# Everything ahead of the experts in one hand-written order: modulation as matmuls, the state-space operators on VectorE, parameters loaded in long rows

## The chip, the core and the metric

One core of a Trainium2 chip runs the whole program. The time is the device time of that core in microseconds (us), the median of three runs. The engines are PE (TensorE matmul; PEld, its weight loads), DVE (VectorE), ACT (ScalarE), POOL (GpSimd) and SP, which here only issues DMAs.

## What is computed

One layer of a hybrid network on 512 latent rows and 256 context rows of 1024 columns, all in float32:

```python
m = silu(cond) @ w_mod + b_mod              # 6 x 1024 columns, for c; the first 2 x 1024 for c_ctx too
h = rmsnorm(x, norm1_g) * (1 + scale1) + shift1
z = h @ w_in                                # 256 columns u, 3 x 768 columns b, c, v
y = concat(s5(u), b * dwconv3(c * v))       # s5: two diagonal complex scans, glu
x = x + gate1 * (y @ w_out)
h = rmsnorm(x, norm2_g) * (1 + scale2) + shift2
# top group of 4, then 2 of its 4 experts: weights and indices from h
x = x + gate2 * sum_e gates[:, e] * ((silu(h @ w1[e]) * (h @ w3[e])) @ w2[e])   # 16 experts
out = rmsnorm(x, final_g)
```

## The kernel before, in words

**Precision.** A float32 product that matters is made of three matmuls of 128 rows by 512 columns (mm3, line 97), for which each operand is split in a high part (ACT, line 74) and a low one (a subtraction on DVE or POOL, line 75).

**Modulation.** w_mod has 6144 columns. The first 2048 (shift and scale of the first norm, for c and c_ctx) come in 16 loads of 512 KB in rows of 512 bytes (load_mod) and are multiplied with 128 by 128 matmuls of 2 columns (line 91, `b,sc`), turned on PE, and make Asc and modT (lines 249 to 252). The other 4096 columns are mod_rows (lines 719 to 751): for each of eight parts q of 512 columns, DVE multiplies half of the eight 128-row blocks by sc and adds them up (line 735), ACT and POOL do the other half (lines 739 to 742), and a matmul with ones (ones_f) sums over the partitions into a row that is the same on all partitions: mx2 (the gate), sh2, A2 (shift and scale of the second norm) and mx5.

**First norm and u.** x is normed and turned on PE, modulated as it leaves PSUM (ACT line 518, DVE line 520), split into H and L; two blocks of w_in give u, for x and for ctx.

**S5 operators.** From lambda, dt, B and C come powers of a_bar (apw), the input operator MinT (12 products and sums of 1024 elements per partition on DVE; cmul, lines 310 to 315), the phasors W (doubling steps on POOL, in s5_tables) and the output operator CA (24 operations of 576 elements on POOL). s5_scan takes u through them: matmuls, products, two scans per direction (lines 638 to 667), readout, gelu and glu.

**Conv blocks.** 18 blocks of 128 columns of w_in, six each of c, v and b: a load, a split (five of the b blocks on POOL), 24 matmuls, and DVE and ACT work on the result (lines 590 to 607).

**Order.** All of this is written as four generators that are advanced in turn (cv_, scan_, mods_, ins_); a scheduler that simulates the program places the instructions on each engine, with a few explicit constraints (issue_after). The expert section alone is in manual order for PE, DVE, ACT and POOL.

**Output projection and router.** wo_mm(n) does 16 steps of 12 matmuls (8 for each half of the columns): w_out is multiplied by mx2 on POOL (line 869), split, used. add_x adds x (line 920). XA = x * A2 (line 954, DVE); the rows go through PE to the logits (line 937); lg (line 966) starts the top-k chain of small DVE operations, which ends in the one-hot matrices OH (line 1009). With those PE gathers expert 0's rows (X0, `bank<-OH,b`), first_parts adds the shift and splits (lines 1056 to 1058). Four operations of 1024 elements (line 1176) scale x for the table td in DRAM, from which the later experts' rows are gathered (POOL, line 1024).

**Experts.** 192 loads of 512 KB go into a ring of 34 slots (load_to), each piece is split (split_to; the first seven among the last conv blocks and the steps of the output projection), each expert takes 72 large matmuls; its result is scattered to yd (POOL, line 1029). Then yd is read back and normed.

Of the kernel before, what the change touches and what calls it, by code (L numbers as in the profile page):

```python
# [7 lines left out]
F32 = mybir.dt.float32  # L8
# [6 lines left out]
CAP = 96  # L15
# [3 lines left out]
def layer_kernel(  # L19
# [79 lines left out]

    R_X = R_MIN = R_SBD = 0  # L100
# [10 lines left out]
    wm_slot = [at(R_RING + 4 * i, [8, 128]) for i in range(8)]  # L111
# [3 lines left out]
    Cr = at(R_SM + 2, [2, 2, 128])  # L115
# [6 lines left out]
    def load_mod(q):  # L122
        m = (q // 4 % 2) * 8 + q // 8 * 4 + q % 4
        D.dma_start(wm_slot[q % 8], dap(w_mod, m * 128, [[6144, 128], [6144 * 128, 8], [1, 128]]))
# [8 lines left out]
    s5_loads = []  # L133
    for ri, src in enumerate((s5_lambda_re, s5_lambda_im)):
        for d in range(2):
            r0 = (ri * 2 + d) * 8
            s5_loads.append((R2[r0:r0 + 8].rearrange("r (a p) -> r a p", a=2),
                             dap(src, d * 1024, [[64, 8], [512, 2], [1, 64]])))
    for g in range(2):
        s5_loads.append((LD[g * 64:(g + 1) * 64], dap(s5_log_dt, g * 8, [[0, 64], [16, 2], [1, 8]])))  # L140
    for ri, src in enumerate((s5_b_re, s5_b_im)):
        for d in range(2):
            for g in range(2):
                s5_loads.append((Bt[g * 64:(g + 1) * 64, ri, d],
                                 dap(src, d * 16384 + g * 8192, [[16, 64], [1024, 8], [1, 16]])))
    for ri, src in enumerate((s5_c_re, s5_c_im)):
        s5_loads.append((Cr[:, ri].rearrange("r d (a p) -> r (d a) p", a=2), dap(src, 0, [[64, 128], [8192, 4], [1, 64]])))
    s5_loads.append((vec2[0:16], dap(b_mod, 0, [[128, 16], [1, 128]])))
    s5_loads.append((vec2[16:24], dap(norm1_g, 0, [[128, 8], [1, 128]])))
    s5_loads.append((vec2[24:26], dap(b_glu, 0, [[128, 2], [1, 128]])))  # L150
    s5_loads.append((vec2[26:44], dap(conv_w, 0, [[128, 18], [1, 128]])))

    def small(n):
        for _ in range(n):
            if s5_loads:
                o_, i_ = s5_loads.pop(0)
                D.dma_start(o_, i_)

    S.dma_start(vec[0:8], dap(c, 0, [[128, 8], [1, 128]]))
    S.dma_start(vec[8:16], dap(c_ctx, 0, [[128, 8], [1, 128]]))  # L160
    load_mod(0)
    load_mod(1)
    small(4)
    load_mod(2)
    small(2)
    load_mod(3)
    small(4)
    load_mod(4)
    load_x(0)
    small(4)  # L170
    load_mod(5)
    load_x(1)
    small(9)
    load_mod(6)
    load_mod(7)
    load_x(2)
# [39 lines left out]
    warm = ct([1, 1], F32, "warm")  # L216
    S.activation(warm, ones_f[0:1, 0:1], AF.Silu)
# [3 lines left out]
    S.activation(sc, b[:, 0:16], AF.Silu)  # L221
    vT = ct([128, 64], F32, "vT")
    b = nb("s")
    tr(b[:, 0:44], vec2)
    V.tensor_copy(vT[:, 16:60], b[:, 0:44])

    mrow = at(R_T, [2, 8, 128], part=2)
    modT = ct([128, 16, 2], F32, "modT")
    Asc = ct([128, 8, 2], F32, "Asc")
    mq = 0  # L230
    for half in range(2):
        for s in range(2):
            b = nb("v")
            for m4 in range(4):
                for k in range(8):
                    mm(b[0:2, m4 * 128:(m4 + 1) * 128], sc[:, k::8], wm_slot[mq % 8][:, k, :], k == 0, k == 7)
                mq += 1
                if mq + 7 < 16:
                    load_mod(mq + 7)
                if mq == 2:  # L240
                    load_x(3)
            V.tensor_copy(mrow[:, s, half * 4:half * 4 + 4].rearrange("p a b -> p (a b)"), b[0:2, :])
        b = nb("v")
        for s in range(2):
            for m4 in range(4):
                tr(b[:, (s * 4 + m4) * 2:(s * 4 + m4) * 2 + 2], mrow[:, s, half * 4 + m4])
# [85 lines left out]
    last_hx = [None]  # L332

    CT = at(R_SM + 2, [2, 2, 8, 16])

    def s5_operators():
# [4 lines left out]
        for d in range(2):  # L341
            for ri in range(2):
                tr(b[:, (d * 2 + ri) * 128:(d * 2 + ri + 1) * 128], Cr[:, ri, d])
        S.activation(CT.rearrange("p a b c d -> p (a b c d)"), b, AF.Copy)
# [43 lines left out]
        V.tensor_mul(qf[:, 1], t[2], t[0])  # L388
        BtF = Bt.rearrange("p r d g h -> p r (d g) h")
# [4 lines left out]
        yield  # L394

        MinT = at(R_MINT, [2, 2, 8, 8, 16])
        mt1 = at(R_V, [8, 8, 16])
        mt2 = at(R_V + 4, [8, 8, 16])
        for d in range(2):
            sl = slice(7, None, -1) if d == 0 else slice(0, 8)  # L400
            sh = [128, 8, 8, 16]
            gs = slice(d * 8, d * 8 + 8)
            pw = [apw[:, ri, gs, sl][:, :, :, None].to_broadcast(sh) for ri in range(2)]
            bv = [bb[:, ri, gs, :][:, :, None, :].to_broadcast(sh) for ri in range(2)]
            with tc.issue_after(last_hx[0].ins):
# [1148 lines left out]
```

## Time and profile before

| | |
|---|---|
| median of three runs | 685.41 us (685.35 to 685.83) |
| the profiled execution | 688.22 us, span 686.5 us |
| busy | PE 595.4 (87%), DVE 538.8 (78%), ACT 357.0 (52%), POOL 276.5 (40%) |
| DMA | 172.26 MB, 251 GB/s over the span |
| granted PE clock, mean | 0.92 |

Busy times are sums over one execution. The program has stages with different limits, so that a share of the whole span says little; the views by stretch and the chain of waits are what is read.

### The profile page before, as it was taken

Reading aid. Unit: us, or ns where it says so; the run is one execution under the profiler, and the core shown is the slowest. Engines: PE = TensorE matmul, PEld = TensorE weight load, DVE = VectorE, ACT = ScalarE, POOL = GpSimd, SP = SyncE. Lnnn points to the kernel's source line nnn. Section 1 sums busy time; section 2 is a strip of 40 time slices with the busy share of each in tenths; the row PEclk is TensorE's granted clock in tenths of the full one; section 3 lists DMA queues with packets and bytes.
Section 4 is the critical chain, followed back from the end, with each engine's and each line's share of the span. In section 5 each row is a group of like instructions: output and inputs, shape, how many; then the busy total and the mean of one; then the engine's idle time right before and its main releaser. Section 6 shows DMA issues by size and latency. Waiting matters only on the chain.

```text
span 686.5 us, 9226 instructions
## 1 busy us (share of the span) xinstructions
PE 595.4 (87%) x3002; PEld 441.8 (64%) x3003; DVE 538.8 (78%) x813; ACT 357.0 (52%) x498; POOL 276.5 (40%) x233
## 2 busy tenths in 40 slices
PE   6776839899787798999979999999999999999970
PEld 3454638677565675687868677777776777777740
DVE  2565997656998774783296899999999999999853
ACT  0325316445333154353113777777777777888631
POOL 4059997875447224442100123333333433332040
PEclk9797788899898799998968999999999999999996
DMA  8999011777569587675977999999999999999445
GB/s 185 217 258 222 2 31 42 201 219 214 154 169 209 134 244 178 224 238 191 354 275 273 326 363 355 362 364 366 365 366 363 365 360 359 359 352 374 133 146 125
DMA packets 111091, 172.26 MB, mean 251 GB/s; under 512 B 14219, under 2 KB 51431, under 8 KB 111039
## 3 DMA queue, kind: packets, MB, share of 16 engines
q1 hardware_dynamic: 106943, 158.68, 72.3%
q0 software_dynamic: 4064, 12.94, 8.5%
q8 instruction: 24, 0.39, 0.2%
q14 instruction: 28, 0.23, 0.1%
q10 hardware_dynamic: 32, 0.01, 0.0%
HBM read 156.53 MB, written 14.02 MB: 248 GB/s over the span
## 4 chain that ended last, share of the span: by engine, by line
DMA 32%; issue 24%; DVE 18%; PE 16%; SPq 3%; ACT 3%; POOL 3%; POOLq 0%; DVEq 0%; ACTq 0%
DMA b<-td,idx 12%; PE bank L97 10%; DMA b<-in_w_mod_dram 7%; PE bank L91 4%; DMA yd<-b,idx 4%; DVE b L75 4%; DMA b<-in_w_in_dram 2%; DVE b L735 2%; DMA b<-in_expert_w_dram 1%; SPq L120 1%; ACT b L74 1%; DMA b<-in_norm_g_dram 1%; PE bank L195 1%; DMA b<-in_ctx_dram 1%; DMA b<-yd 1%
## 5 line engine op out<-in xcount | busy, mean ns | idle before, releaser
L97 PE MATMUL bank<-b,b 128*96 128x512 f32 (+2 forms) x1872 | 458.9, 402 | 22.3 <-DVE b L75 10.8
L97 PEld LDWEIGHTS bank<-b,b 128*96 128x96 f32 (+1 forms) x1872 | 322.4, 177 | 136.7 <-DVE b L75 14.7
L75 DVE TENSOR_TENSOR b<-b,b 128x1024 fp32r<-128x1024 f32 (+2 forms) x249 | 291.3, 1214 | 48.4 <-ACT b L74 46.1
L74 ACT ACTIVATE b<-b 128x1024 fp32r<-128x1024 f32 (+3 forms) x254 | 240.4, 980 | 77.4 <-POOL b L869 23.8
L1024 POOL DMA_INDIRECT b<-td,idx x15 | 18.8, 1255 | 194.5 <-PE bank L195 141.3
L1029 POOL DMA_INDIRECT yd<-b,idx x15 | 69.0, 4600 | 39.1 <-DVE b L1123 38.7
L195 PE MATMUL bank<-ident,b 96*128 96x96 f32 (+4 forms) x343 | 48.6, 279 | 24.9 <-ACT b L503 10.4
L195 PEld LDWEIGHTS bank<-ident,b 96*128 96x128 f32 (+4 forms) x343 | 41.0, 156 | 36.4 <-ACT b L503 10.7
L735 DVE SCALAR_TENSOR_TENSOR b<-b,sc,b 128x512 f32<-128x512 f32 x36 | 32.4, 899 | 25.9 <-DMA b<-in_w_mod_dram 16.8
L740 POOL TENSOR_TENSOR b<-b,b 128x512 f32<-128x512 f32 x21 | 30.8, 1468 | 47.7 <-ACT b L739 36.5
L74 ACT ACTIVATE b<-bank 128x384 fp32r<-128x384 f32 x46 | 22.0, 479 | 37.6 <-PE bank L195 37.6
L91 PE MATMUL bank<-b,sc 128*2 128x128 f32 x256 | 35.2, 302 | 7.1 <-DMA b<-in_w_mod_dram 6.7
L91 PE MATMUL bank<-b,b 128*64 128x96 f32 (+5 forms) x320 | 35.6, 289 | 6.4 <-DVE b L465 5.0
L869 POOL TENSOR_TENSOR b<-b,b 128x512 f32<-128x512 f32 x16 | 22.6, 1416 | 45.5 <-DMA b<-in_w_out_dram 33.3
L91 PEld LDWEIGHTS bank<-b,b 128*64 128x64 f32 (+3 forms) x312 | 27.5, 150 | 14.8 <-POOL b L740 5.4
L739 ACT ACTIVATE b<-b,sc 128x512 f32<-128x512 f32 x21 | 15.2, 723 | 38.2 <-DMA b<-in_w_mod_dram 38.2
L91 PEld LDWEIGHTS bank<-b,sc 128*2 128x2 f32 x256 | 22.8, 93 | 18.2 <-DMA b<-in_w_mod_dram 9.0
L75 DVE TENSOR_TENSOR b<-bank,b 128x384 fp32r<-128x384 f32 x46 | 25.3, 551 | 4.0 <-ACT b L74 3.9
L1123 DVE SCALAR_TENSOR_TENSOR b<-bank,gate,b 96x512 f32<-96x512 f32 x32 | 22.5, 739 | 1.3 <-PE bank L97 1.3
L501 ACT ACTIVATE b<-b 128x1024 f32<-128x1024 f32 x6 | 6.3, 1054 | 31.0 <-DMA b<-in_x_dram 23.7
L310 POOL TENSOR_TENSOR b<-b 128x16 f32<-128x16 f32 (+4 forms) x12 | 5.5, 455 | 30.7 <-DVE Asc L252 29.8
L503 ACT ACTIVATE b<-b,ss 128x1024 f32<-128x1024 f32 x6 | 6.9, 1149 | 20.2 <-DVE ss L213 19.0
(321 smaller groups left out, 492.6 us busy)
## 6 DMA issues: line engine op xcount, KB each, us to landing
b<-in_expert_w_dram SPq DMA_DIRECT2D x192, 512.0 KB
b<-in_w_mod_dram SPq DMA_DIRECT2D x48, 512.0 KB
b<-in_w_in_dram SPq DMA_DIRECT2D x20, 512.0 KB
b<-in_x_dram SPq DMA_DIRECT2D x16, 256.0 KB
b<-in_w_out_dram SPq DMA_DIRECT2D x16, 256.0 KB
td<-b SPq DMA_DIRECT2D x5, 512.0 KB
yd<-b SPq DMA_DIRECT2D x8, 256.0 KB
b<-yd SPq DMA_DIRECT2D x4, 512.0 KB
```

The source lines that it names most:

```text
L74: S.activation(hi, x_, AF.Copy)
L75: return (e or V).tensor_sub(lo, x_, f32(hi))
L91: T.matmul(o, l, r, start=start, stop=stop)
L97: T.matmul(o, l, r, start=start and n == 0, stop=stop and n == 2)
L195: T.transpose(o, i, ident[0:n, 0:n])
L735: V.scalar_tensor_tensor(acc[q], m[:, kk], sc[:, k:k + 1], acc[q], op0=OP.mult, op1=OP.add)
L739: S.activation(m[:, kk], m[:, kk], AF.Copy, scale=sc[:, k:k + 1])
L740: P.tensor_add(acc2, acc2, m[:, kk])
L869: P.tensor_mul(wor[i], wor[i], mx2[h])
L1024: return P.indirect_dma_start(out=xg, out_offset=None, in_=td[:, :], in_offset=bass.IndirectOffsetOnAxis(ap=idx[:, e:e + 1], axis=0), boun ...
L1029: P.indirect_dma_start(out=yd[:, :], out_offset=bass.IndirectOffsetOnAxis(ap=ix, axis=0), in_=src, in_offset=None, bounds_check=639, oob_i ...
L1123: V.scalar_tensor_tensor(yt[:, r], yb[h][0:CAP], gate[:, e:e + 1], mx5[h][0:CAP], op0=OP.mult, op1=OP.mult)
```

## The change

It puts PE, DVE, ACT, POOL and SP in manual order from the start to the end of the experts, so that the order of the text is the order on each engine. Parts of the work move between engines and some loads get longer rows:

- The first 2048 columns of w_mod are loaded with rows of 2 KB and multiplied with 512 columns moving and the conditioning (32 columns wide, two of them used) stationary; block k writes partitions 32 (k mod 4) and up, and `sel` sums the four groups.
- mod_rows: the products and sums on DVE, ACT and POOL become four matmuls per row_unit, each into its own 32 partitions of a bank; a DVE sum with b_mod (row_sum) and a matmul with `sel` (row_wide) per part.
- MinT is cut in steps; phasors and output operator move from POOL to DVE; all splits' low parts are on DVE.
- B, C and the router weights are loaded in long rows and turned or copied on the chip; the small vectors are loaded from ACT's queue, w_glu, norm2_g, u's round trip and the zero stores from POOL's.
- x is turned before the modulation is there and modulated afterwards. Root chains take two row tiles at once.
- w_out times mx2 moves from POOL to DVE, one step ahead; XA moves from DVE to POOL, and X0 is gathered from x itself, with A2 applied in first_parts.
- The scaling of x for td, and the gates, follow behind first_parts on DVE. Expert pieces are split only from there on. w1 and w3 come in rows of 4 KB. The loads ahead of the experts are 9 in the first half of the output projection, 21 by its end, 33 after gather(1).

```diff
-    wm_slot = [at(R_RING + 4 * i, [8, 128]) for i in range(8)]
+    wm_slot = [at(R_RING + 4 * i, [2, 512]) for i in range(8)]
...
+    order_ = tc.manual_schedule(engines={mybir.EngineType.PE, mybir.EngineType.DVE, mybir.EngineType.Activation,
+                                         mybir.EngineType.Pool, mybir.EngineType.SP})
...
-        D.dma_start(wm_slot[q % 8], dap(w_mod, m * 128, [[6144, 128], [6144 * 128, 8], [1, 128]]))
+        D.dma_start(wm_slot[q % 8], dap(w_mod, q % 8 * 128 * 6144 + q // 8 * 512, [[6144, 128], [1024, 2], [1, 512]]))
...
+        for s in range(2):
+            for k in (2 * kp, 2 * kp + 1):
+                mm(mb[s][group(k)], scp[:, k], wm_slot[k][:, s], k < 4, k >= 4)
...
-            cmul(P, W[:, 0, :, n:n + 1], W[:, 1, :, n:n + 1], W[:, 0, :, h:h + 1], W[:, 1, :, h:h + 1],
+            cmul(V, W[:, 0, :, n:n + 1], W[:, 1, :, n:n + 1], W[:, 0, :, h:h + 1], W[:, 1, :, h:h + 1],
...
-                cmul(P, CA[:, d, 0, gl], CA[:, d, 1, gl], pw[0], pw[1], cv_[0], cv_[1], ct1, ct2)
+            cmul(V, CA[:, d, 0, gl], CA[:, d, 1, gl], pw[0], pw[1], cv_[0], cv_[1], ct1, ct2)
...
+    def row_unit(u):
+
+        q, k4 = u // 2, u % 2
+        if k4 == 0:
+            rowb[0] = nb("m")
+        for k in range(4 * k4, 4 * k4 + 4):
+            mm(rowb[0][group(k)], sc[:, k:k + 1].to_broadcast([128, 32]), mslot[k // 2 % 2][:, k % 2], k < 4, k >= 4)
+        row_loads(u + 1)
+
+    def row_sum(q):
+        V.tensor_add(acc[q], rowb[0], acc[q])
...
+    def row_wide(q):
+
+        b = nb("m")
+        mm(b, sel[:, 0:1].to_broadcast([128, 128]), acc[q], True, True)
...
+    for i in range(1, 18):
+        block_split(i + 1)
+        block_mm(i)
+        if i >= 2:
+            run(mods_, 1)
+
+        if i < 6:
+            run(front, (0, 3, 4, 2, 2, 2)[i])
+        block_out(i)
...
-        P.tensor_mul(wor[i], wor[i], mx2[h])
+        V.tensor_mul(wor[i], wor[i], mx2[h])
...
-        V.tensor_mul(XA[i], XR[i], accp[2])
-    load_to(25)
+        P.tensor_mul(XA[i], XR[i], accp[2])
+    load_to(21)
...
-            mm(X0[k // 4][:, k % 4 * CAP:(k % 4 + 1) * CAP], XA[i][:, k * 128:(k + 1) * 128], OH0[i], i == 0, i == 3)
+            mm(X0[k // 4][:, k % 4 * CAP:(k % 4 + 1) * CAP], XR[i][:, chunk(k)], OH0[i], i == 0, i == 3)
```

The order itself changes at two places that matter below. In the conv stretch the output operator stood on POOL (names are buffers; b_4608 is CA, b_288 the powers, b_512 the turned C), of before:

```order
L310 TENSOR_TENSOR b_576_100_954<-b_288_31_333,b_512_18_90 128x576
L311 TENSOR_TENSOR b_576_101_955<-b_288_31_333,b_512_18_90 128x576
L312 TENSOR_TENSOR b_4608_35_337<-b_576_100_954,b_576_101_955 128x576
L313 TENSOR_TENSOR b_576_100_954<-b_288_31_333,b_512_18_90 128x576
L314 TENSOR_TENSOR b_576_101_955<-b_288_31_333,b_512_18_90 128x576
L315 TENSOR_TENSOR b_4608_35_337<-b_576_100_954,b_576_101_955 128x576
```

and the changed kernel has two such groups on DVE within one conv block (L75 is the low part of a later block's w_in, L700 to L707 the block's own result, L847 a row_sum):

```order
L75 TENSOR_TENSOR b_1024_94_610<-b_1024_10_83,b_1024_97_613 128x1024
L326 TENSOR_TENSOR b_576_159_1225<-b_288_40_186,b_512_45_191 128x576
...
L331 TENSOR_TENSOR b_4608_44_190<-b_576_159_1225,b_576_160_1226 128x576
L700 TENSOR_TENSOR b_640_109_752<-b_640_109_752,bank_63 128x512
L706 SCALAR_TENSOR_TENSOR b_512_103_746<-b_640_109_752,vT,b_512_103_746 128x512
L707 SCALAR_TENSOR_TENSOR b_512_103_746<-b_640_109_752,vT,b_512_103_746 128x512
L75 TENSOR_TENSOR b_1024_92_608<-b_1024_8_81,b_1024_95_611 128x1024
L847 TENSOR_TENSOR b_4096_110_755<-bank_67,b_4096_110_755 128x512
```

The operator's operations now stand between two blocks' low parts on the one engine that both need.

In the router, DVE of before scaled x for td (L1176) ahead of the logits' sum (L966), which starts the top-k chain:

```order
L213 TENSOR_SCALAR rs<-rst 128x4
L1176 SCALAR_TENSOR_TENSOR b_1024_123_1987<-b_1024_127_1991,rs,b_1024_7_78 128x1024
...
L966 TENSOR_TENSOR lg<-bank_69,rs 128x80
L1176 SCALAR_TENSOR_TENSOR b_1024_126_1990<-b_1024_130_1994,rs,b_1024_7_78 128x1024
L967 TENSOR_TENSOR lg<-lg,crow 128x80
L973 TENSOR_REDUCE m_2539<-lg 128x20
```

In the changed kernel the same scaling (L1337) stands behind first_parts (L1219) and the gates (26 operations, L1293 to L1334), ahead of the first expert piece's low part (the last row):

```order
L1219 TENSOR_SCALAR b_768_187_2536<-bank_64,AST 128x96 x4
L75 TENSOR_TENSOR b_768_189_2542<-b_768_187_2536,b_768_188_2541 128x384
L1293 TENSOR_TENSOR pe<-lg,m_2466 128x16
...
L1334 TENSOR_TENSOR idx<-idf,b_96_192_2585 96x16
L1337 SCALAR_TENSOR_TENSOR b_1024_114_786<-b_1024_21_107,rs,b_4096_110_755 128x1024
...
L1347 CAST cntI<-cntF 128x17
L75 TENSOR_TENSOR b_1024_198_2635<-b_1024_2_75,b_1024_197_2634 128x1024
```

Ahead of the top-k chain DVE has four operations fewer there, and behind first_parts four more.

## Rows read from the trace of the kernel before

**Rows 1.** Stretches of 20 us, busy per engine, PEclk, DMA share, GB/s
```profile
20.00:40.00 20.00, 14.09 (x85) 8.93 (x85) 13.86 (x132) 6.34 (x9) 1.95 (x8) 0.74 1.08 239
40.00:60.00 20.00, 14.54 (x126) 10.34 (x126) 7.70 (x43) 4.97 (x7) 15.49 (x49) 0.98 1.08 232
60.00:80.00 20.00, 15.68 (x53) 11.71 (x54) 19.28 (x27) 12.40 (x19) 19.14 (x18) 0.60 0.42 110
80.00:100.00 20.00, 10.58 (x51) 8.29 (x49) 20.00 (x16) 1.20 (x2) 19.47 (x10) 0.92 0.09 26
...
400.00:640.00 240.00, 239.98 (x1143) 170.54 (x1142) 231.69 (x249) 186.88 (x219) 81.02 (x26) 1.00 1.04 361
```

**Rows 2.** Groups of instructions to 372 us: busy, mean ns, idle before
```profile
L735 DVE SCALAR_TENSOR_TENSOR b<-b,sc,b 128x512 f32<-128x512 f32 x36 | 32.4, 899 | 25.9 <-DMA b<-in_w_mod_dram 16.8 <-DMA b<-in_b_mod_dram 8.9
...
L310 POOL TENSOR_TENSOR b<-b,b 128x576 f32<-128x576 f32 x4 | 8.3, 2076 | 0.2
...
L314 DVE TENSOR_TENSOR b<-b,b 128x1024 f32<-128x1024 f32 x2 | 4.4, 2183 | 0.0
...
L310 DVE TENSOR_TENSOR b<-b,b 128x1024 f32<-128x1024 f32 x2 | 3.5, 1744 | 0.0
...
L312 DVE TENSOR_TENSOR b<-b,b 128x1024 f32<-128x1024 f32 x2 | 2.4, 1212 | 0.0
```

**Rows 3.** One line, durations ns min/median/max
```profile
L270 DVE SCALAR_TENSOR_TENSOR b<-b,b x12: 165/172/176, 13.0 to 29.5; 128x16 f32<-128x16 f32 x12
```

**Rows 4.** Groups of instructions to 372 us, further shapes
```profile
L91 PE MATMUL bank<-b,ones_f 128*128 128x512 f32 x16 | 8.7, 623 | 4.3 <-POOL b L742 3.5 <-issue 0.8
...
L91 PE MATMUL bank<-b,b 128*64 128x96 f32 x128 | 6.4, 250 | 1.2 <-POOL b L315 1.1 <-ACT b L616 0.2
...
L649 DVE TENSOR_TENSOR_SCAN b<-b,b 128x768 f32<-128x768 f32 x2 | 3.5, 1752 | 0.0
...
L520 DVE TENSOR_SCALAR b<-bank,Asc,modT 128x512 f32<-128x512 f32 x4 | 3.1, 798 | 0.0
...
L639 DVE TENSOR_TENSOR b<-b,b 128x768 f32<-128x768 f32 x2 | 1.9, 945 | 0.0
...
L712 DVE TENSOR_TENSOR b<-b,b 128x512 f32<-128x512 f32 x2 | 1.4, 684 | 0.0
```

**Rows 5.** The chain of waits that ended last: start us, us, what
```profile
67.53 1.13 DVE Asc L252
...
109.82 6.14 PE bank L97 x29
...
339.93 1.37 DVE b L920 x2
...
361.24 9.81 PE bank L91 x64
...
372.12 3.96 PE bank L97 x16
...
652.23 6.22 DMA yd<-b,idx
```

**Rows 6.** Timeline of PE in three stretches: start us, us, what
```profile
120.70 1.04 PE L195 MATMUL bank<-ident,b 128*128 128x128 f32 x8
...
285.08 5.31 PE L97 MATMUL bank<-b,b 128*128 128x512 f32 x22
...
329.62 12.32 PE L97 MATMUL bank<-b,b 128*128 128x512 f32 x53
```

**Rows 7.** Groups of instructions to 372 us, the router
```profile
L1176 DVE SCALAR_TENSOR_TENSOR b<-b,rs,b 128x1024 f32<-128x1024 f32 x4 | 5.0, 1280 | 0.0
L954 DVE TENSOR_TENSOR b<-b,b 128x1024 f32<-128x1024 f32 x4 | 4.9, 1216 | 0.0
```

**Rows 8.** Timeline of all engines about the start of the experts
```profile
374.41 1.23 DVE L75 TENSOR_TENSOR b<-b,b 128x1024 fp32r<-128x1024 f32 x1 [1.00 <-ACT b L74]
```

**Rows 9.** The page, DMA queues: packets, MB, share
```profile
q0 software_dynamic: 4064, 12.94, 8.5%
```

More of the change, by code (lines that the diff above doesn't have):

```diff
@@ L161, in layer_kernel, with w_load @@
+    raw_u = [at(64 + 4 * i, [8, 128]) for i in range(2)]
+    low_u = [atr(64 + 4 * i, [8, 128]) for i in range(2)]
+    hi_u = [atr(72 + 4 * i, [8, 128]) for i in range(2)]
+    def w_load(t, off):
+        D.dma_start(t, dap(w_in, off, [[2560, 128], [2560 * 128, 8], [1, 128]]))
     load_mod(0)
     load_mod(1)
-    small(4)
+    load_bc(Braw, (s5_b_re, s5_b_im))
+    load_bc(Craw, (s5_c_re, s5_c_im))
     load_mod(2)
-    small(2)
     load_mod(3)
-    small(4)
+    load_x(0)
+    load_x(1)
@@ new lines, in row_sum @@
+    def row_sum(q):
+        V.tensor_add(acc[q], rowb[0], acc[q])
+        if q // 2 == 2:
+            P.dma_start(g2, dap(norm2_g, (q % 2) * 512, [[0, 128], [1, 512]]))
+    def row_wide(q):
+        b = nb("m")
+        mm(b, sel[:, 0:1].to_broadcast([128, 128]), acc[q], True, True)
+        if q // 2 == 2:
+            V.scalar_tensor_tensor(acc[q], b, 1.0, g2, op0=OP.add, op1=OP.mult)
+        else:
+            S.activation(acc[q], b, AF.Copy)
+    def mod_rows():
+        for u in range(16):
+            if u % 2 == 0 and u:
+                row_wide(u // 2 - 1)
+            row_unit(u)
+            if u % 2:
+                row_sum(u // 2)
+            yield
+        row_wide(7)
+        yield
@@ L875, in wo_mm, with pieces_ @@
             mm3(psb[h][q], YH[k][:, l], YL[k][:, l], woh[i], wol[i], n % 8 == 0, n % 8 == 7)
-    for n in range(NWO):
-        wo_load(n)
-    load_to(1)
+        wo_load(n + NWO)
+    scan_, mods_, ins_ = s5_scan(), mod_rows(), s5_inside()
+    def pieces_(*gs):
+        for g in gs:
+            yield from g
+    front = pieces_(s5_input(0), s5_input(1), s5_phasors(), s5_output(0), s5_output(1))
+    block_mm(0)
+    block_split(1)
+    run(front, 3)
+    u_context()
+    P.memset(accall, 0.0)
+    P.dma_start(accall[0:1, :], dap(b_mod, 2048, [[4096, 1], [1, 4096]]))
+    row_loads(0)
+    block_out(0)
+    for i in range(1, 18):
[6 more added lines that the diff above has]
+        block_out(i)
+        if i == 1:
+            s5_input_turned(0)
+        elif i == 2:
+            s5_input_turned(1)
+        elif i in (3, 4):
+            run(scan_, 1)
+        elif i == 5:
+            run(ins_, 1)
+        elif i == 6:
+            run(scan_, 2)
+            run(ins_, 9)
+        elif i < 14:
+            run(scan_, 3)
+        else:
+            run(scan_, 1)
+        if i >= 15:
+            wo_load((i - 15) * 2)
+            wo_load((i - 15) * 2 + 1)
+    run(scan_, 99)
+    run(mods_, 99)
+    wo_parts(0)
     for i in range(4):
```

587 lines of the change are left out of this document (313 added, 274 removed).

## The prediction

> **What bounds the kernel now.** I read the stretches first, then the groups of instructions, then the chain of waits. The expert phase is one even stretch: from 400 to 640 us PE is busy 239.98 of 240, DVE 231.69, and DMA is full at 361 GB/s [rows 1]. Three resources are level there, so nothing that the change does before it makes that phase shorter. What is left to win lies ahead of it. There, three different limits follow one another. From 20 to 60 us DMA is full (share 1.08) but moves only 239 and 232 GB/s; from 60 to 100 us it nearly stops (110 and 26 GB/s) while DVE and POOL are both full, 20.00 and 19.47 of the second 20 [rows 1]. The chain has its marks: Asc is there at 67.53, the matmuls of u start at 109.82, the output projection ends at 339.93, X0 runs from 361.24, the experts from 372.12 [rows 5]. I move these marks one by one.
>
> **Up to u.** Sixteen loads of 0.524 MB are 8.4 MB. At the mean of the two slices, 235.5 GB/s, that is 35.6 us; with 2 KB rows, as the expert loads had at 361 GB/s, 23.3 us [rows 1]. DMA thus gives about 12 us, but the mark is then DVE's. Its ordered chain up to the first matmul of u is: 108 small state-space operations at 172 ns [rows 3], 18.6 us from about 10 us, so to 29 (the same group ran from 13.0 to 29.5 before, among other work); two root chains of 15 small operations, 4 us each (2.6 at that price, more where one waits for the other), to 37; six copies of 512 columns out of PSUM at about 0.68 (as the 512 column operation) and the small sums behind the modulation, 5, to 42; six operations of 256 columns for B, 2.4, to 44; eight modulated blocks at 0.798 + 0.684 [rows 4], 11.9, to 56; two low parts of w_in at 1.23 [rows 8], to about 59. So u starts near 59 for 109.82, some 51 us earlier. u itself keeps its length, 109.82 to 120.70 [rows 5, 6], beside which DVE makes the context's parts; the first conv block starts near 72.
>
> **The conv stretch.** I price DVE's list for blocks 0 to 11. The operators that come from POOL took 2.08 us for 576 elements there, and MinT on DVE 1.74 to 2.18 us per 1024 while POOL worked beside it, but 1.21 for the one that ran alone [rows 2]. POOL has almost no arithmetic left in this stretch, so I take 1.21 per 1024 and scale by length: MinT 12 x 1.21 = 14.5; the output operator 24 x 0.68 = 16.3; phasors 42 x 0.172 and 36 longer ones at about 0.3, 18. The scan's operations at their quiet prices (0.945 for 768 elements, 0.684 for 512, 1.752 for a scan [rows 4]): some 33. Twelve low parts at 1.21, 14.5; four blocks each of v and b results, 16 operations at 0.68, 10.9; five row sums, 3.4. Sum 110.6. What it removes from DVE is the 32.4 us of products [rows 2], and from POOL all of its sums. I add 10 us for turns in which DVE waits for PE, and reach block 12 at 72 + 121 = 193. The last six blocks have no operators, so PE sets them: 24 matmuls at 12.32/53 = 0.232 us [rows 6] are 5.6, a row_unit of four matmuls that run together about 1.09, as one 512 column float32 matmul took (8.7 us for 8, two records each [rows 4]): 6.7 x 6 = 40; three row_wide 3.3; readout, gelu, glu some 10. The output projection starts at about 246, for 285.08 [rows 6].
>
> The bounds: with all of it overlapped, PE's own work (18 blocks 101, 16 units 17, row_wide 9, scan and readout some 13) would put the mark at 212; with DVE at the prices beside a busy POOL, half as much again on the operators and the scan (82 us), it would be 287. I take 246, nearer the quiet end, since the prices above were read where POOL was idle.
>
> The four matmuls of a unit go to four different groups of output partitions. That such matmuls run together is seen only for two groups: 128 of 64 columns took 6.4 us, 50 ns each, where one has a length of 250 ns [rows 4]. The Trainium skill, "TensorE: Matmul & The Clock Gate", section "Measured speedup vs the span model", gives 2.38 for three groups 32 columns wide; by its figure a unit is an estimated 1.4 to 1.8 us, and the stretch's PE bound some 10 us longer. No run here shows it for four.
>
> **Output projection and router.** Multiplying by mx2 on DVE takes the place of low parts that have gone; DVE has 1.9 us of work for 2.8 us of matmuls. So it keeps its 339.93 - 285.08 = 54.8 us and ends at 301. Then 21.3 us passed to X0 [rows 5]; four operations of 1.216 and four of 1.280 no longer stand in it [rows 7], 10.0 us, so X0 starts at 312 and ends 9.81 us later at 322 [rows 5]. first_parts takes 2.2: 324.
>
> **A new wait.** Before, the gates were computed beneath X0, and experts began at 372.12, a microsecond behind it; seven pieces had been split long before. Now the order on DVE puts 26 gate operations (24 small ones at 0.172 to 0.21, two of 768 at 0.945), a PE round trip of 1, the four scalings 5.1 and 0.5 for the counts ahead of the first low part of 1.23: 15 us. PE stands still in it. The experts start near 340, 32 us earlier rather than 47. The seven low parts, 8.5 us, also move into a phase in which DVE has 8.3 us to spare in 240 [rows 1]: nothing to 8.5; I take 3, since PE and not DVE was full.
>
> **Sum.** 340 + (686.5 - 372.12) + 3 = 657 us of span, 29.5 less than 686.5. The profiled execution took 688.22, 1.72 over its span, and the median of the runs is 2.8 below it, so I take the difference to the median: 685.41 - 29.5 = 656.
>
> **Rivals.**
> - *The stretch overlaps fully.* The order lets DVE run ahead, PE is the bound from u on, the projection starts at 212: 34 us less, 622. For it: a block's low part stands a block ahead of its matmuls. Against: operators stand between low parts that PE needs next. Chance 0.20.
> - *Loads become the limit of the experts.* 22 loads are out before gather(1), at about 342, 170 behind it: 89.1 MB plus 12.94 MB of gathers and scatters [rows 9] at 361 GB/s [rows 1] are 283 us, to 625, and a last load has some 8 us of matmuls behind it and then the tail of 34.3, from the last scatter at 652.23 [rows 5] to 686.5: 667 of span, 666. Rows of 4 KB speak against it, DMA that idles around 330 for it. Chance 0.12.
> - *Column groups don't run together.* Then the change doesn't do what it says: a unit costs 4 x 1.09, 3.3 more, hidden under DVE up to block 11, bare in six blocks, 20 us: 676. Chance 0.08.
> - *Slower: DVE and PE take turns.* Each engine keeps the text's order, so a DVE operation that waits for PE's result holds up the low part behind it. If PE's time of blocks 0 to 11, 12 x 6.7 = 80 us, lies behind DVE's instead of beside it, the mark moves by up to 70 (10 are in the sum): 726. It decides from 29.5, when 4 of every 10 us of PE are bare; at 5 of 10 the time is 686. For it: low part, operators and a block's result alternate on one queue. Against: the block of slack named above. Chance 0.08.
> - *Moving operators from POOL to DVE gives nothing.* If the two only share one path, each operation costs on DVE what POOL paid, 2.08 per 576: the operators take 34 us more on DVE, which is bound there, and the time is 690. Against it is the row at 1.21. Chance 0.03. The Trainium skill, "Perfetto Trace Analysis", section "Optimizing Scalar/DVE Operations", warns of just that: the two share a read port, so moving work between them might not help; by MinT's rows the trace agrees that they disturb each other, and not that DVE alone is no faster.
>
> **Numbers.** The forecast as it stands has 0.46, its own range 635 to 678 (the projection at 225 to 268); a front that gives nothing and takes nothing has 0.03. A measurement here can tell 0.2%, 1.4 us. Faster: 0.46 + 0.20 + 0.12 + 0.08 = 0.86; slower 0.11; same 0.03. The range for 8 in 10 takes in the full overlap at its edge, the load limit and the serial units, and leaves out the slower cases' upper part: 618 to 684.
>
> **What would show it.** The first matmul of u near 59; the DVE groups of MinT near 1.2 us; matmul starts within a unit a few ns apart; the projection's first matmul between 225 and 270; DVE full and PE idle for some 15 us between X0 and the first expert; from there a period and a tail as before. The forecast is wrong in kind if u starts later than 80, if the expert period lengthens, or if PE and DVE alternate in the conv stretch without either being full.

## The result, and the profile after

The changed kernel takes 801.84 us (801.14 to 808.21, 4 runs) beside 685.62 on the same chip: ratio 1.170, 95% interval 1.164 to 1.177. The forecast was 656; the profiled execution has a span of 799.6 where 657 was forecast, 142.6 more. Here are the marks, with the forecast's and those of before [rows 5, 6].

| mark, us | before | forecast | after |
|---|---|---|---|
| u runs without a stop | 109.82 | 59 | 78.53 |
| first conv block | – | 72 | 99.7 |
| output projection starts | 285.08 | 246 | 331.28 |
| its second half is added | 339.93 | 301 | 387.20 |
| X0 | 361.24 to 371.05 | 312 to 322 | 404.92 to 420.17 |
| experts start | 372.12 | 340 | 437.66 |
| end | 686.5 | 657 | 799.6 |

So 85 us were missed up to the projection, 6.4 in the router, 5.4 in X0, 44.5 in the experts; the projection and the wait behind X0 kept the forecast's length to 1.2 us. The stretches of the kernel after, for [rows 1] (busy us and count of PE, its weight loads, DVE, ACT, POOL; PEclk, DMA share, GB/s):

```profile
40.00:60.00 20.00, 15.41 (x77) 8.91 (x75) 9.89 (x32) 9.57 (x14) 1.49 (x3) 0.69 0.71 190
60.00:80.00 20.00, 5.68 (x21) 4.89 (x22) 10.88 (x19) 7.93 (x12) 3.28 (x11) 0.57 0.24 53
80.00:100.00 20.00, 14.59 (x62) 11.53 (x61) 9.06 (x28) 6.64 (x11) 0.00 (x0) 0.84 0.00 1
...
100.00:300.00 200.00, 154.17 (x834) 110.67 (x833) 121.83 (x211) 43.81 (x78) 24.60 (x35) 0.86 0.43 117
...
405.00:410.00 5.00, 5.00 (x22) 5.00 (x22) 0.58 (x3) 0.00 (x0) 0.00 (x0) 0.50 0.15 58
410.00:415.00 5.00, 5.00 (x23) 5.00 (x23) 0.27 (x1) 1.92 (x5) 0.00 (x0) 0.50 0.00 0
415.00:420.00 5.00, 5.00 (x23) 4.93 (x22) 0.29 (x1) 0.00 (x0) 0.00 (x0) 0.50 0.00 0
...
500.00:700.00 200.00, 186.82 (x845) 129.08 (x845) 176.53 (x190) 140.22 (x168) 26.33 (x21) 0.98 1.01 354
```

From 40 to 100 us no engine is full, and from 100 to 300 PE works 154 of 200 us and DVE 122: no engine is full there either. The experts, where PE was full, have holes (187 of 200 us). What PE and, in one row, ACT waited for from 99 to 331, and DVE from 440 on (us in total, times, longest):

```profile
PE bank L91 <- DVE b L505: 11.6, 1, 11.6
PE bank L91 <- ACT b L731: 10.7, 1, 10.7
PE bank L197 <- ACT b L452: 6.8, 2, 6.5
PE bank L91 <- DMA b<-in_w_mod_dram: 5.6, 4, 3.6
PE bank L197 <- DVE b L799: 5.5, 1, 5.5
PE bank L91 <- DVE b L771: 4.6, 1, 4.6
...
ACT b L701 <- DVE b L700: 33.9, 5, 11.1
...
DVE b L1284 <- DMA b<-in_expert_w_dram: 17.4, 2, 15.8
DVE b L1284 <- DMA b<-yd: 13.3, 1, 13.3
```

The prices, however, came out (groups from 99.7 to 331; busy us, mean ns, idle before): MinT (L426) 1.22 per 1024 where 1.21 was taken, the output operator (L329) 0.76 where 0.68 was. For MinT there was luck in it: the row that I took for the quiet price (L312 of before) did not run alone. It ran at 86.51 and 99.88, and GpSimd worked beside it both times.

```profile
L91 PE MATMUL bank<-b,b 128*64 128x96 f32 (+4 forms) x296 | 37.1, 319 | 28.0 <-DVE b L505 11.6 <-ACT b L731 10.7 <-DVE b L771 4.6
L91 PE MATMUL bank<-b,sc 128*32 128x512 f32 x128 | 20.7, 618 | 5.6 <-DMA b<-in_w_mod_dram 5.6
L91 PE MATMUL bank<-b,sel 128*128 128x512 f32 x16 | 8.2, 596 | 0.9 <-DVE b L847 0.9
...
L329 DVE TENSOR_TENSOR b<-b,b 128x576 f32<-128x576 f32 x4 | 3.0, 758 | 0.1
...
L426 DVE TENSOR_TENSOR b<-b,b 128x1024 f32<-128x1024 f32 x2 | 2.5, 1225 | 0.1
```

The column groups run together: the 128 records of the units took 20.7 us, 1.29 a unit or 0.16 a record, where the records of `sel`, of the same 512 columns but without groups, took 0.51 each. The length of a record alone would not show it, and my sign for two groups in [rows 4] was of that kind: L97's records are 410 ns long and follow one another every 0.25 us (109 us for 432) without groups. By the figure of the Trainium skill, "TensorE: Matmul & The Clock Gate", section "Measured speedup vs the span model", a unit was an estimated 1.4 to 1.8; four groups here are a little better than that, and a little worse than my 1.09.

The timeline shows how the waits come about, in the conv stretch, behind X0 and in the experts (start, us, engine, line, tiles; in brackets the idle time before and who ended it):

```profile
57.17 0.69 DVE L572 TENSOR_TENSOR b<-b,b 128x512 fp32r<-128x512 f32 x1
58.74 0.68 DVE L571 TENSOR_SCALAR b<-b,Asc,modT 128x512 f32<-128x512 f32 x1 [0.88 <-ACT b L570]
...
164.99 0.76 DVE L331 TENSOR_TENSOR b<-b,b 128x576 f32<-128x576 f32 x1
165.66 0.68 DVE L700 TENSOR_TENSOR b<-b,bank 128x512 f32<-128x512 f32 x1
...
166.44 0.72 ACT L701 ACTIVATE b<-b,vT 128x512 f32<-128x512 f32 x1 [11.08 <-DVE b L700]
...
167.55 0.32 ACT L731 ACTIVATE b<-bank 128x192 f32<-128x192 f32 x1
...
167.92 2.83 PE L91 MATMUL bank<-b,b 128*64 128x96 f32 x32 [10.74 <-ACT b L731]
...
392.85 2.23 DVE L1125 TENSOR_TENSOR ss<-ss 128x4 f32<-128x4 f32 x1
...
404.92 15.25 PE L91 MATMUL bank<-OH,b 128*128 128x96 f32 x64 [0.68 <-DVE OH L1171]
429.14 0.80 PE L91 MATMUL bank<-b,b 128*96 128x96 bf16 x8 [8.97 <-DVE b L1321]
437.66 2.87 PE L97 MATMUL bank<-b,b 128*96 128x512 f32 x6 [6.63 <-DVE b L75]
...
500.15 1.60 DVE L1284 SCALAR_TENSOR_TENSOR b<-bank,gate,b 96x512 f32<-96x512 f32 x2 [15.84 <-DMA b<-in_expert_w_dram]
```

At 166 the chain has three queues in it. DVE's product of a v block (L700) stands behind output operators that nobody needs yet (the last is L331); ACT's L701 waits 11.08 us for it; behind L701 on ACT stand the copies L730 and L731 that free a bank for the scan's matmuls; PE waits 10.74 us for these, with the next conv block behind them on its own queue. No operation is slow.

### The profile page after: what moved, and what is told of

It reads as the page before. It is cut to its first block, busy times and chain, and to the rows that moved or that the text cites. A ratio compares the mean times of both kernels' runs of the same rounds, so it can differ in the third digit from the quotient of the medians.

```text
span 799.6 us, 9031 instructions
## 1 busy us (share of the span) xinstructions
PE 635.7 (79%) x3014; PEld 453.0 (57%) x3015; DVE 528.6 (66%) x890; ACT 339.7 (42%) x470; POOL 89.2 (11%) x103
## 5 line engine op out<-in xcount | busy, mean ns | idle before, releaser
L97 PE MATMUL bank<-b,b 128*96 128x512 f32 (+2 forms) x1872 | 463.3, 403 | 42.0 <-ACT b L74 17.9
L97 PEld LDWEIGHTS bank<-b,b 128*96 128x96 f32 (+1 forms) x1872 | 322.5, 178 | 168.8 <-DVE b L75 30.4
L75 DVE TENSOR_TENSOR b<-b,b 128x1024 fp32r<-128x1024 f32 (+2 forms) x238 | 265.0, 1158 | 88.3 <-ACT b L74 84.9
L74 ACT ACTIVATE b<-b 128x1024 fp32r<-128x1024 f32 (+2 forms) x238 | 230.1, 1005 | 53.6 <-DVE b L974 20.0
L91 PE MATMUL bank<-b,b 128*64 128x96 f32 (+7 forms) x384 | 64.8, 423 | 52.3 <-DVE b L505 11.6
L197 PE MATMUL bank<-ident,b 96*128 96x96 f32 (+3 forms) x323 | 50.1, 297 | 31.8 <-ACT b L548 8.4
L197 PEld LDWEIGHTS bank<-ident,b 96*128 96x128 f32 (+3 forms) x323 | 45.8, 193 | 42.8 <-ACT b L548 10.0
L1284 DVE SCALAR_TENSOR_TENSOR b<-bank,gate,b 96x512 f32<-96x512 f32 x32 | 23.8, 744 | 32.4 <-DMA b<-in_expert_w_dram 17.4
L1249 ACT ACTIVATE b<-bank 96x512 f32<-96x512 f32 x16 | 9.5, 595 | 62.1 <-DVE b L1284 61.5
L1190 POOL DMA_INDIRECT yd<-b,idx x15 | 22.5, 1497 | 65.3 <-DVE b L1284 65.3
L75 DVE TENSOR_TENSOR b<-bank,b 128x384 fp32r<-128x384 f32 x46 | 25.3, 550 | 2.5 <-ACT b L74 2.5
L847 DVE TENSOR_TENSOR b<-bank,b 128x512 f32<-128x512 f32 x8 | 5.5, 691 | 29.6 <-PE bank L91 27.8
L91 PE MATMUL bank<-b,sc 128*32 128x512 f32 x128 | 20.7, 618 | 5.6 <-DMA b<-in_w_mod_dram 5.6
L701 ACT ACTIVATE b<-b,vT 128x512 f32<-128x512 f32 x6 | 4.3, 721 | 33.9 <-DVE b L700 33.9
L1117 POOL TENSOR_TENSOR b<-b,b 128x1024 f32<-128x1024 f32 x4 | 9.3, 2355 | 58.1 <-DVE b L1074 58.1
L91 PE MATMUL bank<-OH,b 128*128 128x96 f32 x64 | 15.2, 439 | 0.7 <-DVE OH L1171 0.7
```

What stands on the lines that cost most here:

```text
L74: S.activation(hi, x_, AF.Copy)
L75: return (e or V).tensor_sub(lo, x_, f32(hi))
L91: T.matmul(o, l, r, start=start, stop=stop)
L97: T.matmul(o, l, r, start=start and n == 0, stop=stop and n == 2)
L197: T.transpose(o, i, ident[0:n, 0:n])
L701: S.activation(o, e[:, 1:9], AF.Copy, scale=w3[1])
```

## The experiments

**One tile for the rows.** The change makes the four rows mx2, sh2, A2, mx5 slices of one tile of 4096 columns at 32 to 48 KB. Expert buffers lie in the same place (sil 32, hh 34, the result rows 36, a weight slot 40). Theory A: order is kept for whole tiles, so a result that reads mx5 (L1284) waits for a weight load into A2's old place, and the last expert's pair for the read-back of yd into a slot there.

```
-    accall = at(32, [4096])
-    accp = [accall[:, q * 1024:(q + 1) * 1024] for q in range(4)]
+    accp = [at(32 + 4 * q, [1024]) for q in range(4)]
```

> The changed kernel with mx2, sh2, A2 and mx5 as four tiles of 1024 columns (as before) in place of four slices of one tile of 4096 (POOL clears and loads them one by one). Theory A, one tile: the output step of each expert (L1284) reads mx5, and the order of reads and writes is kept per whole tile where tiles overlap in memory, so it waits for work on other buffers at the same 16 KB (the gated tile, the result rows, a ring slot, the read-back), and that work waits for it. Then the DVE wait of 15.8 us at 484 us goes, the period falls from 18.9 to 17.7 us and the last step loses its 13 us wait: 801.8 - 45 = 757 us, 750 to 765. Rival B, loads: fewer loads were out when the experts began (22 for 31) and the rest came in one burst, and the waits come from full queues: nothing changes by more than 5 us, 795 to 805.

759.39 us, a ratio of 1.106 (1.095 to 1.117). An expert takes 17.92 us instead of 18.89, and the last expert's pair, which had waited 13.3 us for the read-back, waits 0.65 us each for PE. The reverse, one tile in the kernel before:

> The kernel before with its four tiles made slices of one tile of 4096 columns, nothing else. Theory A: its experts get the waits of the changed kernel: a period of 18.9 us for 17.66, the stall and the late last step: 685.4 + 25 to 45, 710 to 732. Rival B: 684 to 690.

730.36, a ratio of 1.063 (1.053 to 1.074), with the same two waits (DVE, experts):

```profile
DVE b L1124 <- DMA b<-yd: 14.1, 1, 14.1
DVE b L1124 <- DMA b<-in_expert_w_dram: 7.1, 2, 4.2
```

Both ways agree: 42.5 us off, 42 to 45 on. That the one tile costs this is shown; that the reason is an order kept for the whole tile is read from the waits, for loads and a read-back whose bytes L1284 does not touch.

**Pieces of the order.** A block's results ahead of the operators (the two statements change places):

```
+        block_out(i)
         if i < 6:
             run(front, (0, 3, 4, 2, 2, 2)[i])
-        block_out(i)
```

> The changed kernel with each conv block's result (block_out) ahead of the operator steps on DVE, for blocks 1 to 5; nothing else. Theory C, head of the queue: PE's waits of 6.5, 10.7 and 11.6 us between 118 and 190 us come from ACT, whose evacuations for PE stand behind an operation that waits for a DVE result queued behind 6 to 24 operator operations. Then the first two go, the third partly: 12 to 20 us less, 782 to 790. Rival D, DVE is simply full there: the waits only move, within 3 us of 801.8.

793.98, 8 less: a part of what was expected. PE's waits of 6.5 and 10.7 us shrank to 1.5 and 5.4, but the 11.7 for L505 stayed, since that stands behind the operators too. Then the gates and slots (L1285 to L1334) ahead of first_parts:

> The changed kernel with the gates and the slot tables on DVE ahead of first_parts, so that they can run beneath the X0 matmuls. Theory E: PE's 17.5 us between X0 and the first expert are that DVE list, and 8.5 us of it leave it: 793, 791 to 795. Rival F: the slot matmuls wait behind X0 on PE anyway, and the rest ends no earlier: 799 to 803.

798.19, 3.6 less where 8.5 was expected. The experts start 11.2 us behind X0 instead of 17.5, but their holes from the one tile grew and took part of it back. Then both, with four tiles, and the modulated inputs written as all of ACT's, all of DVE's products, all differences:

> The changed kernel with four tiles for the rows, and three pieces of its hand order moved at once: a block's results ahead of the operators, the gates ahead of the first expert's parts, the modulated inputs grouped by engine. If the costs stand beside each other, as theory A has it, they add up from 759: -8 (results first), -6 (gates), and about -6 for the grouped inputs, so 735 to 745. If the stalls hide behind one another (rival B: one of them is hidden by TensorE's own work), it stays at 748 or above. In neither case does it come to the 688 of the kernel before.

736.96, theory A: with four tiles the pieces add up, 22.4 us together.

**No hand order at all up to the experts.** The statement that turns the scheduler off moves from the kernel's start to the first expert's split, and leaves SP out, as in the kernel before; the operations are those of the change, with four tiles.

> The changed kernel with four tiles for the rows, and no hand order up to the experts: the scheduler places the same operations, as in the kernel before. Every other edit stays (conditioning rows on TensorE, operators on VectorE, long rows). Theory A (the order written by hand costs most of what is left, because VectorE's and ScalarE's queues hold a result behind operators that nobody waits for): 690 to 725, TensorE idle in the conv stretch under 30 us instead of 48, projection by 300. Rival B (the contents cost: TensorE's own work grew by the conditioning rows and bounds the stretch in any order): 745 or more.

703.00, a ratio of 1.025 (1.018 to 1.032), theory A: 56.4 us of the 74 that were left are the written order, that of the DMA issues on SP included. From 100 to 300 PE is full:

```profile
100.00:300.00 200.00, 197.09 (x1032) 134.67 (x1031) 116.21 (x153) 62.25 (x102) 24.74 (x37) 0.99 0.69 200
```

**Where operations run.** Phasors and output operators back on GpSimd, hand order and four tiles kept (`cmul(V, ...)` to `cmul(P, ...)` in both):

> The changed kernel with four tiles for the rows, phasors and output operators back on GpSimd; all orders stay. GpSimd gets some 66 us (by the rows of the kernel before), VectorE loses some 33 us that stood ahead of block results. Theory A (results wait behind operators on VectorE): 740 to 752, the waits of ScalarE for L700 (33.9 us) at least halved. Rival B (the operators are needed so early that GpSimd's slower ones hold the scan): 759 or more, with a new wait of TensorE for GpSimd's output operators near block 6.

775.13, 15.7 us slower than with them on VectorE: rival B by the number. ACT's wait at L701 fell to 22.8, not by half, and PE stood 38.8 us at L505:

```profile
PE bank L91 <- DVE b L505: 38.8, 1, 38.8
```

The operators' price is only a part of this wait; the rest is the written order again. Behind the last operator (L331) on GpSimd's queue stands a small index table (L493), and DVE needs it ahead of L505:

```profile
198.79 1.40 POOL L331 TENSOR_TENSOR b<-b,b 128x576 f32<-128x576 f32 x1
200.14 0.14 POOL L493 IOTA jk<- 32x16 int32 x1
200.31 3.90 DVE L495 TENSOR_SCALAR kd<-jk 32x16 f32<-32x16 int32 x1 [32.30 <-POOL jk L493]
```

The operators that PE's next matmuls read by the text, those of the first direction, were done at 184.8; PE went on at 205.4. What the operators cost on GpSimd without the table behind them is not shown. The Trainium skill, "Perfetto Trace Analysis", section "Optimizing Scalar/DVE Operations", warns that moving work between these two engines might not help; here VectorE was 15.7 us better, in this order and with that table's wait in the figure. Next, the kernel before with the conditioning rows alone on TensorE:

```
-                    if kk == 0 or q == 7:
-                        V.scalar_tensor_tensor(acc[q], m[:, kk], sc[:, k:k + 1], acc[q], op0=OP.mult, op1=OP.add)
...
+                    mm(rowb[group(k)], sc[:, k:k + 1].to_broadcast([128, 32]), m[:, kk], k < 4, k >= 4)
```

> The kernel before, with only the conditioning rows of the second half taken from VectorE, ScalarE and GpSimd to TensorE (as in the change), placed by its scheduler. TensorE gets 128 records of 618 ns in four column groups, 20.7 us by the trace after, in a stretch of 175 us in which it was busy 156. Theory A (TensorE bounds this stretch, so work that moves to it is paid): projection 5 to 15 us later, 690 to 703. Rival B (VectorE, busy 130 of the 175, and GpSimd bound it, so relief of them shows): projection 10 us earlier, 672 to 680.

703.32, a ratio of 1.025 (1.017 to 1.034): theory A, at its upper end. The second half of the projection is added at 354.9 instead of 339.9. The scheduler's version of the change with these rows off TensorE again:

> The scheduler's version of the changed kernel (703) with the conditioning rows of the second half back on VectorE, ScalarE and GpSimd as in the kernel before; operators on VectorE, long rows and the router stay as changed. Theory A (the conditioning rows on TensorE cost 18 in either kernel, as they did alone in the kernel before): 683 to 688, the projection some 18 us earlier. Rival B (in this order their place on TensorE was an idle one, and VectorE, with the operators too, is now the one that bounds): 697 or more.

707.36, not faster: rival B. From 100 to 300, the kernel before, this run, and the run with the rows added to the kernel before:

```profile
100.00:300.00 200.00, 170.53 (x890) 132.82 (x891) 151.41 (x155) 87.24 (x147) 109.80 (x84) 0.91 0.67 181
```

```profile
100.00:300.00 200.00, 172.30 (x877) 133.04 (x876) 149.91 (x174) 78.27 (x128) 69.75 (x64) 0.91 0.72 198
```

```profile
100.00:300.00 200.00, 183.09 (x946) 122.32 (x947) 99.32 (x123) 62.39 (x109) 62.85 (x53) 0.94 0.61 165
```

With the rows off, PE is busy 172 of 200 us and DVE 150: neither is full, and yet the stretch is no shorter. PE's waits in it are spread over DVE and ACT, the longest sum 5.4 us; no single bound shows. With the rows and the operators both off (and contiguous columns, below):

> The scheduler's version with contiguous columns, the conditioning rows off TensorE, phasors and output operators on GpSimd, and four more pieces of expert weights loaded early. Theory A (with the rows off TensorE it was VectorE that bound the stretch, busy 38 of 40 us at 180 to 220, and 33 us of operators leave it): the projection 15 us earlier than in the run with the rows off (707), X0 at 7.4 to 10, 672 to 686. Rival B (the chain of operators, slower on GpSimd, holds the scan): 695 or more.

700.67, a ratio of 1.023 (1.018 to 1.028): rival B by the number. The stretch was 4 us shorter, but DVE is still busy 150 of 200 us, GpSimd now 103, and the longest waits of PE are for the scan's states on DVE (9.1 us, of 33 in which PE waited for DVE, ACT or GpSimd). Rows and operators on or off, in all of the scheduler's versions of the change the projection's second half is added between 336.8 and 342.1, where the kernel before has 339.9.

**The stride of four.** The long rows put row 4p + j on partition p, so x is read in every fourth column. Undone in the reordered version (737):

```
-        return slice(q // 4 * 512 + q % 4, q // 4 * 512 + 512, 4)
+        return slice(q * 128, q * 128 + 128)
```

> The reordered version of the changed kernel (737) with the stride of four taken out: columns k*128 to k*128+128 for X0, the turned rows and the experts' columns, router and expert weights loaded in the rows of the kernel before. Theory A (a weight load of every fourth column is slower: 190 instead of 140 ns for 96 rows at full clock, and TensorE's clock stays at half during X0): X0 7.4 to 10 us instead of 15.25, the expert period 17.66 instead of 17.92, 725 to 730. Rival B (X0's clock comes from the idle time before it, the period from longer rows in the loads): X0 stays at 15, 735 to 740.

731.88, a ratio of 1.067 (1.065 to 1.069): between the two theories by the time, theory A by its signs. X0 took 9.54 us and an expert 17.68. The run also takes the long rows out of the loads, but the expert's 0.24 us are on PE itself: the eight transposes of an expert's inputs took 0.83 us where they took 1.09 with the stride. The transposes' weight loads in the experts, with the stride (the run with four tiles) and in the kernel before (mean ns of one behind the busy time):

```profile
L197 PEld LDWEIGHTS bank<-ident,b 96*128 96x128 f32 x152 | 19.9, 190 | 3.3
```

```profile
L195 PEld LDWEIGHTS bank<-ident,b 96*128 96x128 f32 x148 | 15.1, 140 | 4.0
```

In X0 the granted clock rose from half (1.2 of 2.4 GHz) to nearly full after 4 us with contiguous columns, after 6.3 us of idle PE ahead of it:

```profile
385.00:390.00 5.00, 4.32 (x24) 4.22 (x21) 3.86 (x22) 0.42 (x2) 0.00 (x0) 0.50 0.50 180
390.00:395.00 5.00, 5.00 (x45) 5.00 (x45) 2.27 (x4) 1.92 (x5) 0.00 (x0) 0.97 0.00 0
```

With the stride it stayed at 0.50 for all of its 15.25 us. More warm-up products, in the run with the rows off:

> As the run with the rows off TensorE, with 44 warm-up products before X0 instead of 22. Theory A (X0's 15.25 us at half clock come from TensorE's idle stretch of some 3 us before it): the clock stands at full in X0, 8 to 10 us, 5 to 7 us less than without. Rival B (the clock in X0 does not depend on these products): X0 stays at 15 us, and the time is the same or up to 3 us more where the products reach beyond the gates.

709.77, X0 at 15.25 us as before. The scheduler put most of the products ahead of the last logits, so that PE was still idle for 3.5 us ahead of X0; by itself this run doesn't decide, but the run above had more idle time and the faster X0.

**The router in the kernel before.** X0 from XR, A2 as a column, XA behind the one-hot rows:

> The kernel before with one piece of the change, the router: X0 is computed from XR itself, A2 enters the first expert's inputs as a column, and the four products XA (4 x 1216 ns on VectorE, ahead of the gates before) stand behind the one-hot rows. Theory A (VectorE's chain sets the time from the last row sums to X0): 4.9 us shorter there, X0 between 345 and 358, 679 to 683. Rival B (X0 takes longer when it starts after a longer idle of TensorE, as in the kernel after, where its 64 records ran at half clock for 15.25 us): 15 instead of 9.8 us, 685 to 688.

695.34, slower than either theory, with X0 from 354.2 and only 7.38 us long. In it XA stands behind a load of an expert's weights into A2's place, so that its rows of td hold other numbers. With the load behind the products:

> The kernel before with X0 from XR, A2 as a column, and the four products XA behind the one-hot rows, the load into A2's place behind them. Theory A (the products were 4.9 us of the chain to X0): 679 to 683, beside 685 to 688 for the kernel before. Rival B (VectorE then does them while the gates wait for it, and the experts wait for their gather): within 1 us of the kernel before.

694.85, a ratio of 1.011 (1.005 to 1.017): neither theory, it is slower, though X0 starts at 353.3, 8 us earlier. The rows of td are written over XR, and X0 now reads XR. In the kernel before these rows (L1176) ran ahead of X0; here they stand behind it and behind the products, and so VectorE comes late to the first expert's second half (L1059) and to the gates. PE waits for both, for the gates by way of the second expert's gather (timelines, before and this run):

```profile
351.54 3.68 DVE L1176 SCALAR_TENSOR_TENSOR b<-b,rs,b 128x1024 f32<-128x1024 f32 x3
```

```profile
363.51 3.67 DVE L1177 SCALAR_TENSOR_TENSOR b<-b,rs,b 128x1024 f32<-128x1024 f32 x3
...
368.38 8.34 PE L97 MATMUL bank<-b,b 128*96 128x512 f32 x26 [6.72 <-DVE b L1059]
...
387.86 2.18 PE L195 MATMUL bank<-ident,b 96*128 96x96 f32 x12 [5.86 <-DMA b<-td,idx]
```

The remedy tried is to write them over XA, with XA on GpSimd or on VectorE:

```
-        V.scalar_tensor_tensor(XR[i], XA[i], rs[:, i:i + 1], accp[1], op0=OP.mult, op1=OP.add)
+        V.scalar_tensor_tensor(XA[i], XA[i], rs[:, i:i + 1], accp[1], op0=OP.mult, op1=OP.add)
```

> The kernel before with the router from XR, the rows of td written over XA instead of XR, and the products XA on GpSimd behind the one-hot rows. Theory A (the rows waited for X0's reading of XR): td stored before 367 instead of 369, the gather some 5 us earlier than in the run with the rows in XR, TensorE's wait of 5.9 us for it gone, 679 to 686. Rival B (the wait is for the gates, which are no earlier): 690 or more.

> As the run before, with the products XA on VectorE. Theory A: td stored by 364, but the gates 5 us behind the products, 683 to 690. Rival B: 690 or more.

688.19 and 690.61, ratios 1.003 (1.001 to 1.005) and 1.007 (1.004 to 1.009): better than with the rows in XR, and still not faster than the kernel before. The first lies between its two theories, the second is rival B. On GpSimd the wait for the gather fell to 1.35 us, nearly as expected, but the scheduler put the rows ahead of the gates again, so X0 started at 357.3: what one gains the other pays. On VectorE the rows were written by 362.4, and PE still waited 6.4 us for the gather, which left just behind the slot indices:

```profile
374.76 0.18 DVE L1174 TENSOR_TENSOR idx<-idf,b 96x16 int32<-96x16 f32 x1
...
375.91 1.77 POOL L1025 DMA_INDIRECT b<-td,idx  x1 [42.98 <-PE bank L97]
```

So with the products on VectorE it is the gates, late on VectorE's queue, that hold the gather, and not the place of the rows.

**The change without its faults.** The scheduler's version with contiguous columns and 26 instead of 22 early loads, and the same with td's rows over XA:

> The scheduler's version (703) with contiguous columns and four more pieces of expert weights loaded early; rows stay on TensorE, operators on VectorE. Theory A: 5 us at X0, 4 us over the experts, up to 7 us where TensorE waited for the second gather: 687 to 694. Rival B (the gather waits for the stores of td in any order): 694 to 699.

> The scheduler's version with contiguous columns (695), the rows of td written over XA. Theory A: the rows at 357 to 362, under X0, instead of 367 to 373, the gather by 378, the wait of 5.2 us gone, 688 to 691. Rival B: 694 to 696.

695.07, a ratio of 1.012 (1.009 to 1.014), just inside rival B: X0 fell from 15.2 to 10.5 us and an expert to 17.68, but the wait for the gather stayed at 5.2. The gather left at 383.0, 8.8 us behind the indices, so here it was not the gates that held it. Then 686.09 beside 686.50, 0.999 (0.997 to 1.002), some 2 us better than expected: X0 starts 2.7 us later, behind td's rows, and yet the experts gain, since PE no longer waits for the gather:

```profile
359.65 9.66 PE L91 MATMUL bank<-OH,b 128*128 128x96 f32 x64 [0.60 <-DVE OH L1163]
...
370.64 11.13 PE L97 MATMUL bank<-b,b 128*96 128x512 f32 x47 [0.69 <-DVE b L1211]
381.61 0.82 PE L192 MATMUL bank<-ident,b 96*128 96x96 f32 x8
```

No version beat the kernel before. Taken away one after the other, the 116 us are: one tile 42, the written order 56, the stride (with four early loads) 8, td's rows behind X0 9. The figures come from several chips, on which the kernel before had medians of 685 to 688.6, so each holds to some 2 us; that of td's rows is the price in the scheduler's version, where the experts come soon after X0.

## Why the prediction was wrong, step by step

- **Up to u, "u starts near 59".** The list of DVE's work was right in size: the small operations ended 4 us later than I had them, at 33.3 for 29, and what follows took 6 us less. But I summed one engine's list as if it never waited. From 36 us on, DVE waited 21 us in 13 pieces for a bank or a copy (3.24 and 1.01 for transposes, 4.07 and 3.67 for the modulation's columns, six times 0.88 at the modulated inputs, as at 58.74 in the timeline: ACT's part of a block waits for DVE's difference of the block before). 59 and 21 make 80, for 78.53. The blocks are slices of one tile, and the differences are written over it, so this may be the whole tile's order once more; no run takes it by itself. Another 8 went between u and the first block, where ACT and DVE take turns over the context's banks.
- **"PE's own work would put the mark at 212", 140 us.** PE was busy 183 us between 99.7 and 331, at a mean granted clock of 0.88. The scan, the readout and the transposes are 45 (the row of 296 above, and 7.8) where I had 13: I had priced the 128 records of one shape [rows 4] and passed over the other forms of that group, and the context's matmuls (5.9). The blocks are 109 for 101, the units 20.7 for 17. So the rival "the stretch overlaps fully" could not give 622: the scheduler's run does overlap, PE at 197 of 200, and ends the stretch where the kernel before does.
- **"I add 10 us for turns in which DVE waits for PE".** Both waited: DVE 37 us for PE (L847, L856 and L700), and PE 48 us, mostly for ACT and DVE. PE's 183 busy and 48 idle us are the 231.6 that the stretch took, where I had 174. The slow rival had this mechanism, two engines' queues in one order, at a chance of 0.08; ACT as the third queue in the chain it had not. What spoke against it, a block of slack, holds for low parts alone; results, evacuations and the operators have none. Its threshold was reckoned wrong: 4 of every 10 us bare are 0.4 x 80 - 10 = 22, so it decides at 5. Two of the three signs that I had named for a forecast wrong in kind came: the expert period rose from 17.66 to 18.89, and neither PE nor DVE was full in the conv stretch; u, at 78.53, stayed just under 80.
- **The router, "10.0 us".** The eight operations did leave the chain, but the four products moved to GpSimd, and beside them two steps of small DVE work took 2.23 and 2.42 us, some 4 us more than without. DVE also stood idle 1.7 us for a turned row, where before the products had filled its time; 17.7 us instead of 11.3.
- **X0, "9.81 us later".** Forecast as moved unchanged; the stride made it 15.25.
- **"A new wait", 15 us and first_parts 2.2.** Right: 17.5 between X0 and the experts.
- **The experts, "I take 3".** 44.5, of which 42 are the one tile, which the diff shows and I read as a shorter way to write four rows. With four tiles the phase from the first expert on is 320.6 for 314.4, 6 more: 3.8 by the stride (15 times 0.25); that the rest is the 3 of the low parts is not shown.

Nothing bore out the rival on loads: DMA moved 354 GB/s in the experts, and with four tiles PE is full at 200 of 200.

## What to carry to other kernels

A written order must be costed as several queues at once: for each operation that another engine waits for, count what stands ahead of it on its own queue, then what stands behind its reader on the reader's queue. Work that moves to the busiest engine can be paid nearly in full (18 of 20.7 us with the rows on PE in the kernel before), and taking it off again can give nothing back (707 for 703), so each direction needs its own run. A scheduler's order that keeps PE full is hard to beat by moving single pieces (703 for 737). Before joining buffers that are placed by hand into one tile, or before a stage reads a buffer that the next writes, list everything that shares the bytes.

## What was not expected of the hardware

- A weight load of every fourth column costs 190 ns for 140 (96 rows, full clock), and 64 float32 products with such loads ran 15.25 us at a granted clock of 0.50 to the end, while contiguous ones came to 0.97 after 4 us. Why the clock stays down with the stride is open.
- Small VectorE operations beside GpSimd products of 1024 columns: three of 4 columns took 4.58 us together in the run with rows and operators on, for 0.31 without. The last ended at 349.58, when the four products on GpSimd did (340.23 and 9.32). In the run with the operators on GpSimd, two of 16 columns (L495, L496) took 3.9 and 3.8 us, until a memset of 4096 columns on GpSimd ended at 204.2.

```profile
345.00 4.58 DVE L200 TENSOR_SCALAR rst<-ss 128x4 f32<-128x4 f32 x3
```

- GpSimd itself is quicker in a quiet stretch: 1.16 to 1.40 us for 576 elements in the run with the operators on it, while VectorE stood idle, for 2.08 beside a busy VectorE [rows 2].

```profile
L327 POOL TENSOR_TENSOR b<-b,b 128x576 f32<-128x576 f32 x4 | 4.7, 1164 | 0.0
```
